# Routing and layer hand-over of a two-layer decoder trunk: where the expert choice keeps its operands, how many tiles it takes at once, in which order the first expert's work is issued, and which engine makes the next mixer's low parts

## The chip, the cores and the metric

One core of one Trainium2 chip. The metric is device time in microseconds of one execution, the median of several runs; lower is better. The engines' names in the profile are PE (TensorE), DVE (VectorE), ACT (ScalarE), POOL (GpSimd) and SP (SyncE, which here issues the weight loads).

## What is computed

Two layers over x of 512 tokens by 1024, float32. In each layer a mixer (attention of several kinds, ending in an output projection), a LayerNorm, a mixture of 16 experts of which every token uses two, and a second LayerNorm. The part that the change touches most is the choice of experts between the first LayerNorm and the experts:

```python
x = layer_norm(ALPHA * x + mix, ln_g[l, 0], ln_b[l, 0])
aff = jax.nn.sigmoid(xt @ router_w)                       # [512, 16]
sel = aff + router_b
grp_score = lax.top_k(sel.reshape(-1, 4, 4), 2)[0].sum(-1)   # best two of four, summed
g_mask = one_hot(top_k(grp_score, 1))                        # the best group
_, e_idx = lax.top_k(where(e_mask, sel, -inf), 2)            # two experts in it
w = take_along_axis(aff, e_idx); w = w / w.sum(-1)
for e in range(16):
    h = silu(xt @ w_gate[e]) * (xt @ w_up[e])
    y = y + gates[:, e:e + 1] * (h @ w_down[e])
x = layer_norm(ALPHA * x + y, ln_g[l, 1], ln_b[l, 1])
```

## The kernel before

**Number format.** Every product is made of three TensorE products of high and low parts (`mm3`): high by high, low by high, high by low. Of each weight unit of 128 by 1024, ACT writes the high part `wh` (L182, a cast) and DVE or POOL the low part `wl`, weight minus high part (L183).

**Tiles.** The 512 tokens are four tiles of 128. Tiles 0 and 1 lie in one buffer, 2 and 3 in another.

**Routing, in each layer.** `out_proj` makes, for each tile and each half of the 1024 columns, 12 matmuls of 128x512 (`half_proj`) into one of two PSUM buffers `ps_a`. DVE adds them to the tile (L572), takes LayerNorm statistics (L573), PE transposes the half (L577), ACT copies it (L579) and PE multiplies it by the router's weights (L581). `tile_ln` then finds one over the standard deviation in ten tiny DVE steps, scales the logits (L587, L588), takes the sigmoid on ACT (L589), and applies the LayerNorm: ACT centres and scales (L590), POOL multiplies by gamma and adds beta (L252, L253; of the last tile DVE does 256 of the columns), and POOL's queue writes the tile to two places in DRAM: x1d (L592), from which the experts' rows are gathered, and yd (L595), to which results are added.

The string ROUTE_ORDER sets the order in which the program is written: before, `y0 l0 y1 l1 y2 l2 y3 l3 r02 r23 r34`, where y is a tile's projection, l its LayerNorm, and r a choice for a range of tiles. A choice (`choose`, L414 to L455) is some 17 DVE steps on scores in SBUF; `slots` (L468 to L480) counts, with PE, which place in its expert's list each token gets, and compares these places with 0 to 95 (L480); `first_rows` (L483 to L491) collects the rows of the first expert by matmuls from the tiles in SBUF. Each engine executes its own instructions in the order in which a scheduler put them at build time; an instruction that waits holds up all that stand behind it on its engine.

**Experts.** `moe` takes the collected rows out of PSUM (`put_rows`), finds for all experts which tokens fill their places (`after_slots`, L494 to L530: the indices idx for the gathers, a one-hot matrix oht that only the last expert needs, a flag that an expert overflowed, weights), gathers rows of the next experts from x1d (L1109) and runs the 16 experts: gate, up, silu times up (L1146), transpose, down, scatter to yd. Weight chunks of 1 MB are loaded by SP's queue (L1101) in the order of the program. The first 16 (AHEAD) go to buffers that are free, or come free, before the experts begin. Later ones use a ring of buffers.

**Hand-over to the next layer.** In `moe`'s tail TAIL_ORDER sets the order: for each tile p adds the last expert's part (L1255), c squares (ACT, L1263), n finds one over the standard deviation (L212 to L228), m and e apply the LayerNorm (L1271, L1276), t transposes the tile for the next mixer. The next mixer's input weights arrive in four units of 128x968; ACT makes their high parts and POOL their low parts (`ksplit(..., G)`, L880, which calls L183).

## Time and profile before

| | |
|---|---|
| runs | 1184.47, 1179.41, 1177.62 us, median 1179.41 |
| profiled execution | 1178.62 us, of which the span is 1176.7 |
| PE busy | 1084.6 us (92%) |
| DVE busy | 938.5 us (80%) |
| ACT busy | 758.4 us (64%) |
| POOL busy | 240.9 us (20%) |
| mean granted TensorE clock | 0.956 |

The span is the time between the first and the last instruction. PE works for 92% of it, so a gain has to come out of the stretches in which PE stands or runs at the lower clock. In the page's 40 slices (29 us each) these are at the routing of layer 0 (slices 9 and 10), the hand-over (slice 20) and the routing of layer 1 (slices 29 and 30). Times in the text below are microseconds from the span's start.

### The profile page before, as it was taken

What the parts mean: (1) busy time and instruction counts of PE and PEld (TensorE: products, weight loads), DVE (VectorE), ACT (ScalarE), POOL (GpSimd) and SP (SyncE); (2) the same over time, 40 slices, a digit from 0 to 9 for tenths busy, and PEclk for the clock granted to TensorE, in tenths of its full rate; (3) what the DMA queues carried; (4) which work ended last, traced back from release to release, by engine and by line L of the source; (5) the groups of instructions that cost most, each with busy time, mean ns of one, the idle gap of its engine ahead of it and who ended that gap; (6) DMA issues with size and microseconds to landing.
All of it is one profiled execution on the core that took longest, in us unless ns stands there. A gap on an engine that the chain in (4) does not pass through costs nothing. (4 is left out here: it accounts for less than half of the span.)

```text
span 1176.7 us, 16647 instructions
## 1 busy us (share of the span) xinstructions
PE 1084.6 (92%) x5775; PEld 810.7 (69%) x5775; DVE 938.5 (80%) x1871; ACT 758.4 (64%) x1221; POOL 240.9 (20%) x199
## 2 busy tenths in 40 slices
...
GB/s 209 118 37 53 99 66 143 203 277 317 306 340 360 349 344 242 350 354 302 219 1 69 71 23 72 109 95 119 302 281 298 335 351 349 345 246 357 368 294 141
DMA packets 139756, 262.24 MB, mean 223 GB/s; under 512 B 11847, under 2 KB 28263, under 8 KB 139664
## 3 DMA queue, kind: packets, MB, share of 16 engines
...
q8 instruction: 47, 0.77, 0.3%
...
## 5 line engine op out<-in xcount | busy, mean ns | idle before, releaser
L183 DVE TENSOR_TENSOR wl<-wraw,wh 128x1024 fp32r<-128x1024 f32 (+1 forms) x422 | 503.0, 1218 | 73.2 <-ACT wh L182 63.9
L182 ACT CAST wh<-wraw 128x1024 fp32r<-128x1024 f32 (+3 forms) x436 | 445.8, 1039 | 148.6 <-PE ps_s L197 62.3
L195 PE MATMUL ps_s<-wh,m 128*96 128x512 f32 (+1 forms) x528 | 207.6, 393 | 1.7 <-ACT m L200 1.7
L196 PE MATMUL ps_s<-wl,m 128*96 128x512 f32 (+1 forms) x528 | 205.8, 390 | 0.6 <-DVE wl L183 0.6
L197 PE MATMUL ps_s<-wh,m 128*96 128x512 f32 (+1 forms) x528 | 204.6, 388 | 0.3 <-DVE m L201 0.2
L197 PEld LDWEIGHTS ps_s<-wh,m 128*96 128x96 f32 x528 | 85.5, 162 | 35.6 <-DVE m L201 1.3
L195 PEld LDWEIGHTS ps_s<-wh,m 128*96 128x96 f32 x528 | 85.8, 163 | 34.5 <-ACT m L200 2.1
L196 PEld LDWEIGHTS ps_s<-wl,m 128*96 128x96 f32 x528 | 85.6, 162 | 32.4 <-DVE wl L183 0.8
L195 PE MATMUL ps_a<-wh,hH 128*96 128x512 f32 x256 | 102.5, 400 | 0.5 <-ACT hH L200 0.5
L196 PE MATMUL ps_a<-wl,hH 128*96 128x512 f32 x256 | 101.2, 395 | 0.8 <-DVE wl L183 0.8
L197 PE MATMUL ps_a<-wh,hL 128*96 128x512 f32 x256 | 99.9, 392 | 0.0
L1184 POOL DMA_INDIRECT yd<-m,idx x30 | 53.1, 1770 | 188.5 <-ACT m L1183 187.5
L195 PE MATMUL ps_a<-wh,XH 128*128 128x512 f32 (+2 forms) x224 | 88.7, 396 | 2.5 <-ACT wh L182 1.3
L197 PE MATMUL ps_a<-wh,XL 128*128 128x512 f32 (+2 forms) x224 | 87.6, 391 | 2.1 <-DVE XL L201 2.1
L196 PE MATMUL ps_a<-wl,XH 128*128 128x512 f32 (+2 forms) x224 | 86.7, 387 | 0.0
L1109 POOL DMA_INDIRECT m<-x1d,idx x30 | 33.1, 1105 | 255.3 <-PE ps_t L1120 225.6
L197 PE MATMUL ps_a<-XH,wl 128*128 128x512 f32 x160 | 64.7, 405 | 0.3 <-DVE wl L183 0.3
L196 PE MATMUL ps_a<-XL,wh 128*128 128x512 f32 x160 | 64.9, 406 | 0.0
L195 PE MATMUL ps_a<-XH,wh 128*128 128x512 f32 x160 | 64.6, 404 | 0.0
L358 ACT ACTIVATE p<-p,nm 128x256 f32<-128x256 f32 (+3 forms) x96 | 50.6, 529 | 18.5 <-DVE nm L353 9.5
L377 ACT COPY pT<-ps_t 128x512 f32<-128x512 f32 (+2 forms) x88 | 43.5, 517 | 28.2 <-PE ps_t L374 27.3
L197 PEld LDWEIGHTS ps_a<-wh,hL 128*96 128x96 f32 x256 | 41.3, 161 | 18.0
...
## 6 DMA issues: line engine op xcount, KB each, us to landing
...
```

The source lines that it names most:

```text
L182: first(A.copy(hv, w))
L183: first(eng.tensor_tensor(out=lv, in0=w, in1=hv.bitcast(F32), op=ALU.subtract))
L195: T.matmul(o, lh, rh, start=first, stop=False)
L196: T.matmul(o, lh, rl, start=False, stop=False)
L197: T.matmul(o, ll, rh, start=False, stop=last)
L358: A.activation(out=pt[h], in_=(pt if bias else Sp)[h], func=AF.Exp, bias=nm[:, h:h + 1], scale=(slopes[0][h] if slopes else 1.0), accum_ou ...
L377: A.copy(d_, s_)
L1109: G.indirect_dma_start(out=xg_of[e], out_offset=None, in_=x1d[:, :], in_offset=bass.IndirectOffsetOnAxis(ap=idx[:CAP, e:e + 1], axis=0), b ...
L1184: G.indirect_dma_start(out=yd[:, :], out_offset=bass.IndirectOffsetOnAxis(ap=idx[:CAP, e:e + 1], axis=0), in_=yos[e % 2], in_offset=None, ...
```

## The change

- **Choice.** The scores, their sums with the bias, the group sums and the chosen indices lie in an unused part of the PSUM bank of the logits (`scratch`), so that in the choice and the slots no DVE step reads two tensors from SBUF (a column of one value for each partition may be there besides). The sum with the bias is made twice, once to PSUM and once to SBUF, and so is the sigmoid. The compare of places is one TENSOR_SCALAR for each tile.
- **Order of routing.** ROUTE_ORDER is `y0 l0 y1 l1 y2 l2 c03 y3 s03 l3 r03`: one choice for tiles 0 to 2 stands ahead of tile 3's second add; nine of the twelve matmuls of a tile's second half stand behind the logits of the half before. Then comes tile 3's choice by itself.
- **LayerNorm.** Tiles 0 and 1 get their statistics from an add that also sums and from a squaring pass on ACT. Tile 3's LayerNorm is done on DVE in two halves (`centre` and `whole`), placed between the steps of its choice; POOL and ACT do nothing for it, and LN1_DVE is gone. In the one-column case the tiny steps of `rsqrt` are TENSOR_SCALAR with two column operands.
- **First expert.** Its gate's high parts are made behind tile 3's sigmoid and its low parts one by one between `whole` and `put_rows` (before: in the routing, between the choices). `after_slots` is cut in three: `slot_tokens` (indices) in the middle of the first gate, `slot_weights` behind the first expert, `for_the_end` (oht, flag) in expert 4.
- **Buffers.** Chunk 7 (second half of expert 1's up weights) is loaded into the buffer of the first gate's second chunk, and is the last of AHEAD. On SP's queue it stands behind the two loads into the buffers of the tiles; before it stood ahead of them. The router's folded weights are made at the end of the mixer and not in the routing.
- **Hand-over.** The next mixer's four low parts are made by DVE behind tile 0's `e` (`w00 w01 w10`, then `w11`), not by POOL; the steps on ACT keep their order.

Tile 2's second half on DVE in layer 0, before, in the order of the engine (L439 to L450 are steps of the choice of tiles 0 and 1; L572 is the add):

```order
L430 TENSOR_REDUCE gm<-pr 128x2
L439 TENSOR_TENSOR gs<-gs,gm 128x8
L440 TENSOR_TENSOR gs<-gs,desc_121 128x8
L441 TENSOR_REDUCE gm_2680<-gs 128x2
L442 TENSOR_TENSOR gs<-gs,gm_2680 128x8
L443 TENSOR_TENSOR sel<-gs,sel 128x32
L448 MAX rm_2686<-sel 128x8 x2
L450 MAX_INDEX ri_2687<-rm_2686,sel 128x8
L572 TENSOR_TENSOR xr_130<-xr_130,ps_a 128x512
L450 MAX_INDEX ri_2687<-rm_2686,sel 128x8
L573 BN_STATS st<-xr_130 128x6
L452 CAST rf_2692<-ri_2687 128x4
```

After: the end of the choice of tiles 0 to 2, then tile 3's second add (L625), slots and the start of its statistics:

```order
L468 TENSOR_TENSOR sel<-gs,ps_s 128x48
L473 MAX rm_2604<-sel 128x8 x3
L475 MAX_INDEX ri_2605<-rm_2604,sel 128x8 x3
L476 CAST ps_s<-ri_2605 128x6
L477 TENSOR_TENSOR O<-io_119,ps_s 128x96
L480 TENSOR_REDUCE M<-O 128x48
L625 TENSOR_TENSOR xr_130<-xr_130,ps_a 128x512
L503 SCALAR_TENSOR_TENSOR sl<-ps_s,M 128x48
L626 BN_STATS st<-xr_130 128x6
L506 TENSOR_SCALAR oh_2320<-slot_117,sl 128x96 x3
L253 BN_AGGR mv<-st 128x2
```

The add of tile 2's second half no longer stands behind a choice; tile 3's stands behind one of three tiles.

The end of the last choice on DVE in layer 0, before (L455 ends it, L480 compares places, L500 to L506 belong to the indices, L201 is the low part of the first expert's rows):

```order
L455 TENSOR_TENSOR M<-O 128x16
L498 TENSOR_TENSOR R<-O,recc 128x128
L478 SCALAR_TENSOR_TENSOR sl<-ps_s,M 128x16
L519 TENSOR_REDUCE flags<-ps_t 128x1
L480 TENSOR_TENSOR oh_2324<-slot_117,sl 128x96
L500 TENSOR_TENSOR pt<-O,sl 128x128
L513 TENSOR_SCALAR eq<-slot_117,sl 128x96
L502 TENSOR_REDUCE pos<-pt 128x8
L506 TENSOR_SCALAR oh<-slot_117,pos 128x96 x4
L460 TENSOR_TENSOR gt<-O,aff 128x128
L201 TENSOR_TENSOR m_2843<-ps_o,m_2843 128x384
L506 TENSOR_SCALAR oh<-slot_117,pos 128x96
```

After (L480 ends the choice, L676 is `centre`, L681 `whole`, L192 a low part of the first gate, L211 that of the rows, L524 the start of the indices):

```order
L480 TENSOR_REDUCE M<-O 128x16
L676 SCALAR_TENSOR_TENSOR xr_130<-xr_130,mv,lnt 128x512
L503 SCALAR_TENSOR_TENSOR sl<-ps_s,M 128x16
L506 TENSOR_SCALAR oh_2320<-slot_117,sl 128x96
L681 SCALAR_TENSOR_TENSOR xr_130<-xr_130,rs_o,lnt 128x512
L192 TENSOR_TENSOR wl<-wraw_2761,wh 128x1024
L681 SCALAR_TENSOR_TENSOR xr_130<-xr_130,rs_o,lnt 128x512
L211 TENSOR_TENSOR m_2788<-ps_o,m_2788 128x384
L192 TENSOR_TENSOR wl<-wraw_2761,wh 128x1024
L211 TENSOR_TENSOR m_2788<-ps_s,m_2788 128x384
L192 TENSOR_TENSOR wl<-wraw_2763,wh 128x1024
L524 TENSOR_TENSOR pt<-O,sl 128x128
```

The four low parts of the gate and half of tile 3's LayerNorm now lie behind the last choice, and the indices behind three of the low parts.

The hand-over on DVE between the layers, before (L214 to L228 are the last steps of the inverse root, L1276 is `e`, L1271 `m`, L201 the low part of the transposed tile):

```order
L214 TENSOR_TENSOR rs_c<-rs_r 128x2
L215 TENSOR_TENSOR rs_c<-rs_c,rs_h 128x2
L228 SCALAR_TENSOR_TENSOR rs_o<-rs_c,rs_r 128x2
L1276 SCALAR_TENSOR_TENSOR xr_5573<-xr_5573,rs_o,lnt 128x1024
L1271 SCALAR_TENSOR_TENSOR xr_5573<-xr_5573,ls,lnt 128x1024
L201 TENSOR_TENSOR XL_5685<-ps_t,XH_5683 128x4x128
L201 TENSOR_TENSOR XL_5686<-ps_t,XH_5684 128x4x128
L1276 SCALAR_TENSOR_TENSOR xr_5573<-xr_5573,rs_o,lnt 128x1024
```

After (L243 to L245, L1426 and L1421 are the same steps, L1444 the low parts of weights):

```order
L224 TENSOR_TENSOR rs_c<-rs_r 128x2
L225 TENSOR_TENSOR rs_c<-rs_c,rs_h 128x2
L245 SCALAR_TENSOR_TENSOR rs_o<-rs_c,rs_r 128x2
L1426 SCALAR_TENSOR_TENSOR xr_5503<-xr_5503,rs_o,lnt 128x1024
L1444 TENSOR_TENSOR wl<-wraw,wh 128x968 x3
L211 TENSOR_TENSOR XL_5628<-ps_t,XH_5626 128x4x128
L211 TENSOR_TENSOR XL_5629<-ps_t,XH_5627 128x4x128
L1444 TENSOR_TENSOR wl<-wraw,wh 128x968
L1421 SCALAR_TENSOR_TENSOR xr_5503<-xr_5503,ls,lnt 128x1024
L1426 SCALAR_TENSOR_TENSOR xr_5503<-xr_5503,rs_o,lnt 128x1024
```

Four low parts have come to DVE between tile 0's and tile 1's `e`; on POOL none is left there.

The diff, cut to what the steps below touch:

```diff
-AHEAD = (2, 3, 4, 0, 1, 5, 6, 8, 9, 10, 12, 13, 7, 14, 11, 15)
-LN1_DVE = (0, 0, 0, 256)
+AHEAD = (2, 3, 4, 0, 1, 5, 6, 8, 9, 10, 12, 13, 14, 11, 15, 7)
...
-ROUTE_ORDER = "y0 l0 y1 l1 y2 l2 y3 l3 r02 r23 r34"
-TAIL_ORDER = ("p00 p10 / p01 c0 p11 c1 m0 n02 e0 m1 t0 e1 p20 p21 c2 t1 p30 p31 c3 m2 n24 e2 m3 t2 e3 t3",
+ROUTE_ORDER = "y0 l0 y1 l1 y2 l2 c03 y3 s03 l3 r03"
+TAIL_ORDER = ("p00 p10 / h0 | h1 p01 c0 p11 c1 m0 n02 e0 w00 w01 w10 t0 w11 m1 e1 p20 p21 c2 t1 p30 p31 c3 m2 n24 e2 m3 t2 e3 t3",
...
+    def scratch(p):
+        return (p[:, 0:64].rearrange("p (t e) -> p t e", e=NE), p[:, 64:128].rearrange("p (t e) -> p t e", e=NE),
+                p[:, 128:144].rearrange("p (t g) -> p t g", g=4), p[:, 144:152].rearrange("p (t c) -> p t c", c=2))
...
-        V.tensor_tensor(out=sel, in0=aff[:, ts_], in1=rb.unsqueeze(1).to_broadcast([128, n, NE]), op=ALU.add)
-        sg = sel.rearrange("p t (g j) -> p (t g) j", j=4)
+        for t in (selp, sel):
+            V.tensor_tensor(out=t, in0=affp, in1=rb.unsqueeze(1).to_broadcast([128, n, NE]), op=ALU.add)
+        sg, sp = (t.rearrange("p t (g j) -> p (t g) j", j=4) for t in (sel, selp))
...
-        V.tensor_tensor(out=pr[:, :, 0:2], in0=sg[:, :, 0:2], in1=sg[:, :, 2:4], op=ALU.add)
+        V.tensor_tensor(out=pr[:, :, 0:2], in0=sg[:, :, 0:2], in1=sp[:, :, 2:4], op=ALU.add)
...
-        return V.tensor_tensor(out=oh0[:, t0:t1], in0=slot1.unsqueeze(1).to_broadcast([128, n, CAP]),
-                               in1=sl[:, t0:t1, 0:1].to_broadcast([128, n, CAP]), op=ALU.is_equal)
+        for i in range(t0, t1):
+            oh = V.tensor_scalar(oh0[:, i, :], slot1, sl[:, i, 0:1], None, op0=ALU.is_equal)
+        return oh
...
+                o = half_proj(rows[c], oH, oL, g, i, end.get("lg") if main and c else None)
...
+        n = NT - 1
+        with tc.issue_after(end["u"].ins):
+            c0 = centre(0)
+        with tc.issue_after(c0.ins):
+            chosen = choose(n, NT, sc)
+        with tc.issue_after(chosen.ins):
+            c1 = centre(1)
+        with tc.issue_after(c1.ins):
+            oh = slots(sl, oh0, n, NT)
...
-            rows += ksplit(ahead.pop(0) if ahead else latent_load(kh), 2, G)
+            rows += ([(hv[:, j, :], lv[:, j, :]) for _, hv, lv in ahead.pop(kh) for j in range(2)] if ahead else
+                     ksplit(latent_load(kh), 2))
...
-                t = xo.tile([128, 2048], F32, name="wraw3", tag=dict(e=eH, E=eL, l=lL, x=lH)[t])
+                t = xo.tile([128, 2048], F32, name="wraw3", tag=dict(e=eH, E=eL, l=eL, x=lH)[t])
...
-        g0 = [ksplit(load("g", 0, c), 2) for c in range(2)]
-        m2 = xo.tile([128, 2, D], F32R, name="m2", tag=eL)
+        m2 = xo.tile([128, 2, D], F32R, name="m2", tag=lL)
...
-        for c in range(2):
-            put_rows(c, ps2[c])
-        after_slots(sl, oht, flag)
-        for e in (1, 2):
-            gather(e)
+        in_turn(lambda: route["whole"](0))
+        route["rows"](0)
+        low_part(0)
+        in_turn(lambda: route["whole"](1))
+        route["rows"](1)
+        route["x1"]()
+        in_turn(lambda: put_rows(0, ps2[0]))
+        low_part(1)
+        in_turn(lambda: put_rows(1, ps2[1]))
+        low_part(2)
+        found = []
+        def between():
+            with tc.issue_after(last_mm[0].ins):
+                in_turn(lambda: found.extend(slot_tokens(sl, route["room"])) or found[0])
+            low_part(3)
+            for i in (1, 2):
+                gather(i)
...
+            if e == 4:
+                with tc.issue_after(act_op[0].ins):
+                    for_the_end(sl, oht, flag)
...
+        def rest(kh, u):
+            w, hv, lv = early_rows[kh][u]
+            keep(V.tensor_tensor(out=lv, in0=w, in1=hv.bitcast(F32), op=ALU.subtract))
```

## Rows read from the trace of the kernel before

**Rows 1.** Busy time of the engines in stretches of 10 us of layer 0: the routing (first two rows) and the experts (last two). The columns are the stretch, its length, the busy time and count of instructions of PE, PEld, DVE, ACT and POOL, then the granted clock, the mean busy share of the DMA engines and GB/s.

```profile
240.00:250.00 10.00, 7.14 (x35) 6.03 (x34) 7.96 (x32) 1.53 (x2) 4.31 (x4) 0.81 0.96 379
...
260.00:270.00 10.00, 6.95 (x43) 6.86 (x43) 8.78 (x40) 1.34 (x2) 5.02 (x4) 0.67 0.95 335
...
440.00:450.00 10.00, 10.00 (x50) 7.17 (x49) 9.45 (x12) 8.49 (x12) 1.00 (x1) 1.00 0.87 279
450.00:460.00 10.00, 10.00 (x48) 7.03 (x47) 9.20 (x9) 8.66 (x11) 1.59 (x1) 1.00 0.46 134
```

**Rows 2.** Timeline of DVE in the routing of layer 0 and its first expert: start, duration, engine, line, operation, operands; in brackets the idle time ahead of it and what ended it.

```profile
239.07 1.73 DVE L419 TENSOR_TENSOR sel<-aff,rb 128x32 f32<-128x32 f32 x1
...
240.92 2.38 DVE L424 TENSOR_TENSOR pr<-sel 128x16 f32<-128x16 f32 x1
...
245.24 0.67 DVE L572 TENSOR_TENSOR xr<-xr,ps_a 128x512 f32<-128x512 f32 x1
...
256.16 0.18 DVE L478 SCALAR_TENSOR_TENSOR sl<-ps_s,M 128x32 f32<-128x32 f32 x1
...
267.48 0.16 DVE L419 TENSOR_TENSOR sel<-aff,rb 128x16 f32<-128x16 f32 x1
...
270.10 0.17 DVE L455 TENSOR_TENSOR M<-O 128x16 f16<-128x16 f16 x1
...
271.74 0.17 DVE L478 SCALAR_TENSOR_TENSOR sl<-ps_s,M 128x16 f32<-128x16 f32 x1 [1.27 <-PE ps_t L518]
...
271.95 0.26 DVE L480 TENSOR_TENSOR oh<-slot,sl 128x96 f32<-128x96 f16 x1
272.13 0.28 DVE L500 TENSOR_TENSOR pt<-O,sl 128x128 f32<-128x128 f16 x1
...
276.61 0.56 DVE L201 TENSOR_TENSOR m<-ps_s,m 128x384 fp32r<-128x384 f32 x1 [0.23 <-ACT m L200]
...
289.62 0.68 DVE L1146 TENSOR_TENSOR sg<-sg,ps_s 96x512 f32<-96x512 f32 x1
```

**Rows 3.** Timeline of POOL in the same stretch.

```profile
240.83 2.44 POOL L253 TENSOR_TENSOR xr<-xr,lnt 128x1024 f32<-128x1024 f32 x1
...
254.29 3.31 POOL L253 TENSOR_TENSOR xr<-xr,lnt 128x1024 f32<-128x1024 f32 x1
...
265.58 1.86 POOL L253 TENSOR_TENSOR xr<-xr,lnt 128x768 f32<-128x768 f32 x1
...
268.33 0.53 POOL L595 DMA_DIRECT2D yd<-xr  x1
279.15 1.08 POOL L1109 DMA_INDIRECT m<-x1d,idx  x1 [10.29 <-DVE eq L528]
```

**Rows 4.** Timeline of PE in the same stretch.

```profile
245.97 0.91 PE L577 MATMUL ps_t<-ident,xr 128*128 128x128 f32 x4 [2.86 <-DVE xr L572]
...
248.39 1.72 PE L581 MATMUL ps_s<-rwgb,yT 128*128 128x16 f32 x8
...
264.11 0.27 PE L514 MATMUL ps_t<-ident,eq 128*96 128x128 f32 x1
...
267.70 1.99 PE L491 MATMUL ps_o<-oh,xr 128*128 128x96 f32 x8 [3.05 <-DVE sel L419]
...
272.36 2.00 PE L491 MATMUL ps_o<-oh,xr 128*128 128x96 f32 x8 [0.62 <-DVE oh L480]
274.14 1.91 PE L491 MATMUL ps_s<-oh,xr 128*128 128x96 f32 x8
...
276.24 0.77 PE L195 MATMUL ps_s<-wh,m 128*96 128x512 f32 x1
```

**Rows 5.** Timeline of all engines at the hand-over from layer 0 to layer 1.

```profile
574.08 9.74 POOL L183 TENSOR_TENSOR wl<-wraw,wh 128x968 fp32r<-128x968 f32 x4 [12.10 <-ACT wh L182]
...
574.36 3.03 DVE L1271 SCALAR_TENSOR_TENSOR xr<-xr,ls,lnt 128x1024 f32<-128x1024 f32 x1 [3.16 <-ACT sq L1263]
575.34 0.19 ACT L1263 ACTIVATION_READ_ACCUMULATOR sq<-xr,ls 128x1 f32 x1
577.31 2.18 DVE L219 TENSOR_SCALAR rs_v<-ls 128x2 f32<-128x2 f32 x1
...
585.11 1.28 DVE L1276 SCALAR_TENSOR_TENSOR xr<-xr,rs_o,lnt 128x1024 f32<-128x1024 f32 x1
...
586.54 1.94 PE L275 MATMUL ps_t<-ident,xr 128*128 128x128 f32 x8 [14.32 <-DVE xr L1276]
...
589.75 1.27 DVE L1276 SCALAR_TENSOR_TENSOR xr<-xr,rs_o,lnt 128x1024 f32<-128x1024 f32 x1
...
597.53 0.17 DVE L219 TENSOR_SCALAR rs_v<-ls 128x2 f32<-128x2 f32 x1
...
599.32 1.28 DVE L1276 SCALAR_TENSOR_TENSOR xr<-xr,rs_o,lnt 128x1024 f32<-128x1024 f32 x1
```

**Rows 6.** The page's group of the low parts made by DVE: busy time, mean ns of one.

```profile
L183 DVE TENSOR_TENSOR wl<-wraw,wh 128x1024 fp32r<-128x1024 f32 (+1 forms) x422 | 503.0, 1218 | 73.2 <-ACT wh L182 63.9
```

**Rows 7.** What SP's queue waited for at the weight loads (L1101) between 226 and 300: us in total, times, longest.

```profile
SPq L1101 <- DMA yd<-xr: 10.3, 1, 10.3
```

**Rows 8.** Timeline of all engines in layer 1, at the places that answer to 245.97 and 289.62 of layer 0.

```profile
834.72 0.66 PE L577 MATMUL ps_t<-ident,xr 128*128 128x128 f32 x4 [2.98 <-DVE xr L572]
...
878.59 0.68 DVE L1146 TENSOR_TENSOR sg<-sg,ps_s 96x512 f32<-96x512 f32 x1
```

254 lines of the change are left out of this document (176 added, 78 removed).

## The prediction

> **What bounds the kernel now.** I read first the stretches of 10 us [rows 1]. In the experts PE is busy for 10.00 of 10 us at the full clock, so nothing that happens beside them shortens them. In the routing PE is busy for 7.14 and 6.95 of 10, at a granted clock of 0.81 and 0.67. There the timelines of DVE, POOL and PE are laid side by side [rows 2 to 4]. The reader is to see three things. First, the add of tile 2's second half (L572 at 245.24) stands on DVE behind a choice that was held up: L419 took 1.73 and L424 2.38, where an undisturbed L419 takes 0.16 [rows 2]. L424 ends at 243.30, POOL's L253 at 243.27 [rows 2, 3]. Both held steps read two tensors from SBUF; L478 at 256.16, which reads PSUM and one tensor from SBUF, took 0.18 in the middle of a POOL step (254.29 to 257.60). PE waited 2.86 us for that add and then ran the logits at the low clock: 1.72 for eight [rows 4]. Second, DVE begins the last choice only at 267.48, just after POOL has finished tile 3 (267.44) [rows 2, 3], and PE stands for 3.05 [rows 4]. Third, from the end of that choice (270.27) to the first gate product (276.24) everything is a chain: slots, the last tile's rows for the first expert, their split. At the hand-over PE stands for 14.32 us [rows 5], since DVE's steps are held while POOL makes four low parts from 574.08 to 583.82. So DVE's queue sets the time at all three places.
>
> **The change part by part.** Times are those of the trace before; the steps that I place are estimates.
>
> Routing of layer 0. Without a choice ahead of tile 2's add the 2.86 us go, and tile 2's logits end at 250.1 - 2.9 = 247.2. Two scalings and a sigmoid later, at about 248.5, the choice of three tiles starts. The choice of one tile took 267.48 to 270.27, 2.8 us [rows 2]; three tiles add four searching steps, one sum and some width, which I put at 1.3: it ends at 252.6. Tile 3's second add stands behind it on DVE, and behind that add PE's transposes and logits; PE, which has nine matmuls in hand, runs dry at about 250.4 and stands for about 2.5 us. Because a stop of 2.86 was followed by the low clock, I reckon with that clock behind this one. Add, slots, statistics and the ten tiny steps of the root (1.75 undisturbed, 597.53 to 599.28 [rows 5]) bring tile 3's scores to about 257.3 and the last choice to 258.0, with half of `centre` ahead of it. It takes 2.9, to 260.9. From the choice's end to the slots there are 1.5 us (270.27 to 271.74), with the other half of `centre` hidden in them; compare 0.26 and `whole` 0.7 give 263.4. The rows of the last tile take 2.0 and 1.9 on PE [rows 4]; the first gate product comes at 267.4 instead of 276.24. POOL's LayerNorm of tile 3, which ended at 267.44, is no longer in the way; its two halves on DVE cost 0.7 each, of which one lies in a wait.
>
> First expert. Now DVE is the bound, because the gate's four low parts have moved behind the choice. From 263.4: four low parts of the gate at 1.22 [rows 6] 4.9, the second `whole` 0.7, the rows' low parts two at 0.56 [rows 2] 1.1, the indices (three steps at 0.28, two of 128x384 at about 0.56, and a wait of some 1.0 for PE's eight small matmuls) 3.0, four low parts of up 4.9, about 1.0 of waits for ACT: 15.6, to 279.0. The last unit's matmuls add 1.5: the product L1146 starts at about 280.9 with some slack, against 289.62 [rows 2]. I take a gain of **8.5 us**. The bound below the chain is PE: 48 matmuls, of which it does some 50 in 10 us where nothing else holds it [rows 1], so not before about 278.5, a gain of 11. The bound above is 5: steps held once more, and a late gather.
>
> Two waits are new here. POOL's gather for expert 1 needs the indices (about 272.5, before 278.7) and tile 3's rows in DRAM, which POOL's queue now writes at about 266 (yd at 268.33 before [rows 3]). SP waited 10.3 us for such a write [rows 7]. I place the gather at 275 and its landing at 279; the rows are wanted at 281, so it costs nothing, with 2 us of cover. And the compares of places, as TENSOR_SCALAR, stand on DVE ahead of tile 3's statistics while POOL still works on tile 2. TENSOR_SCALAR steps are not safe: one of 128x2 at 577.31 took 2.18 beside POOL [rows 5]. Held at worst once, they cost up to 2.4; POOL should end tile 2 near 254.7, just as they are due, so I take 0.5, which is in the slack above.
>
> The Trainium skill (SBUF — State Buffer, "Who interferes with whom") says that a DVE step with at most one SBUF input stays clear of GpSimd, but that tensor_scalar can enter a mode that takes the shared ports and then blocks. The trace agrees with both halves (0.18 for L478, 2.18 for L219); by it the compares would wait for POOL, and the sum would be up to 3 us worse over both layers than with none held.
>
> The Trainium skill also speaks against putting the choice in PSUM: Perfetto Trace Analysis, "Optimizing Scalar/DVE Operations", gives about 60 ns of access overhead for DVE on SBUF and about 125 on PSUM. Here L478, which reads PSUM, took 0.17 and L419 from SBUF 0.16, so the trace doesn't bear it out for reads; writes to PSUM no row shows. By the skill's figure some 18 steps in each layer would cost 65 ns more, an estimate of 1.2 us a layer, and the sum would come out at 1161.
>
> Layer 1. The same chain: from PE's stop to the product are 43.9 us (834.72 to 878.59 [rows 8]), in layer 0 43.65. I take the same 8.5.
>
> Hand-over. `m` started at 574.36 and the squares end at 575.53; undisturbed, the root runs to 577.4 instead of 585.0, and `e` of tile 0 to 578.7 instead of 586.4: 7.7 earlier. But then four low parts stand on DVE. At 1.22 x 968/1024 = 1.15 each they cost 4.6, of which part lies in waits for the transposes' split (about 0.9 before). Tile 1's `e` ends at about 587.0 against 591.0, and the same chain follows to tile 2's `e` (599.32). I take **4.0**. Bounds: 7.7 - 4.6 = 3.1, and 6, the gain of the first products, if what follows catches up. The casts on ACT stay ahead of the squares as before.
>
> Added to the experts. The one-hot matrix and the flag are made in expert 4, where PE has no idle time: eight small matmuls and transposes, 0.27 long at 264.11 but overlapping [rows 4]; between 0.3 and 1.5, I take **0.5 a layer**. The squares of tiles 0 and 1 on ACT cost nothing: ACT is busy for 1.53 of 10 [rows 1]. The fold of the router's weights lies at the mixer's end, beside PE's work.
>
> Weights. Expert 0 starts 8.5 us earlier, and the loads must follow. In the experts the DMA engines are full but for 440 to 460, with shares of 0.87 and 0.46 [rows 1]: 1.3 + 5.4 = 6.7 us in which they had no free buffer. That is the stream's slack; the missing 1.8 comes out of the lead of some chunks. I cost it at nothing.
>
> Sum: -8.5 - 8.5 - 4.0 + 1.0 = -20.0 against the profiled execution's 1178.6 (span 1176.7): 1158.6. The runs' median is 0.8 higher; I say **1159**.
>
> **The rivals.** (a) The loads don't follow. If the stretch from 460 on is bound by the DMA and not by buffers, both layers end as before and only the hand-over is left: 1178.6 - 4 + 1 = 1176. Against it: PE is busy for 10.00 of 10 while the DMA pauses. (b) The choice is held after all, because a DVE step that writes PSUM or reads a column beside POOL waits as L424 did. A choice of three tiles beside POOL's four steps would lose up to 4 us a layer: 1158.6 + 8 = 1167. (c) All goes better: the clock stays high behind PE's shorter stop and DVE keeps up: 2.5 more a layer and 2 at the hand-over, 1151. (d) Slower: chunk 7. On SP's queue it now stands behind the load into tile 2 and 3's buffer, and that one waits for the write of tile 3's rows. The write starts at about 266 and lands some 11 us later, 277.4; two loads of 1 MB at some 340 GB/s [rows 1] take 6.2, so chunk 7 lands at 283.6. It is wanted at about 286.5 (first expert's end 281 plus a gate of 5.5). From a landing of the write at 280.3 on, each us costs one in each layer; the kernel gets slower than before when the write takes 13 us more. At 26 us instead of 11 it would be 12 late: 2 x (12 - 8.5) - 4 + 1 = +4, 1183. (e) The change doesn't do what it says, PE's three stops stay: 1178.
>
> **How the numbers follow.** My forecast 0.69, (a) 0.06, (b) 0.10, (c) 0.09, (d) 0.04, (e) 0.02. The forecast's own bounds are 5 to 11 a layer, 3.1 to 6 at the hand-over and 0.3 to 1.5 of added work: 1151 to 1168. The range takes in those and most of (b) and (c): 1150 to 1170. About 0.5% (6 us) is what a measurement of this kernel can tell from no change; faster by more than that are my forecast, (b) and (c), 0.88; within it (a) and (e), 0.08; slower (d), 0.04.
>
> **What would show it.** Right: no DVE step of the choice over 0.4 us while POOL works; the last choice on DVE 9 to 10 us earlier relative to tile 2's transposes; first gate product and L1146 8 to 9 us earlier in both layers; PE's stop at the hand-over 6 to 8 us instead of 14.32; rows of PE in expert 4 longer by about 0.5. Wrong: a choice step of 2 us, PE idle ahead of the first expert's matmuls waiting for DVE by more than 3 us in all, ACT or DVE waiting for a weight load in expert 1, or a wait of expert 1's transposes for the gather.

## The result and the profile after

The changed kernel took 1193.56 us in the median of 4 runs (1188.42 to 1199.26), the kernel before 1179.14 beside it; the ratio is 1.0106, with a 95% interval of [1.0078, 1.0133] (it compares runs taken beside each other, here and below, and isn't the quotient of the medians, which is 1.0122). The forecast was 1159, with a range of 1150 to 1170: the sign was wrong. The profiled execution is the longest of the four, 1199.26 (span 1197.1), so its stages add up to more than the median shows. One of the nine runs of e9 below took 1757.1 us at a granted clock of 0.55; it is in none of the figures.

Spans of the two traces, cut at the same events. "Routing" runs from the first transposes of tile 0's new rows (L577, now L630) to the first gate product of expert 0; "first expert" from there to the product of activation and up of expert 1 (the second L1146 of a layer, now L1257).

| us | before | after | difference |
|---|---|---|---|
| start to the routing of layer 0 | 222.07 | 224.46 | +2.4 |
| routing, layer 0 | 54.17 | 48.83 | -5.3 |
| first expert, layer 0 | 27.82 | 40.42 | +12.6 |
| other experts of layer 0 | 253.98 | 254.34 | +0.4 |
| hand-over and mixer of layer 1 | 255.80 | 253.88 | -1.9 |
| routing, layer 1 | 49.94 | 50.71 | +0.8 |
| first expert, layer 1 | 29.26 | 38.95 | +9.7 |
| other experts of layer 1 | 252.29 | 254.24 | +1.9 |
| end | 31.37 | 31.27 | -0.1 |

So the loss lies in the two first experts. Stretches of 10 us in layer 0, columns as in [rows 1]:

```profile
250.00:260.00 10.00, 5.01 (x22) 4.46 (x23) 5.11 (x33) 1.80 (x4) 7.16 (x7) 0.61 0.33 130
...
270.00:280.00 10.00, 8.14 (x35) 6.32 (x35) 8.20 (x15) 2.51 (x4) 1.05 (x2) 0.66 0.83 257
...
290.00:300.00 10.00, 5.11 (x32) 3.91 (x31) 5.93 (x12) 5.09 (x7) 5.15 (x3) 0.83 1.04 351
```

In two of these stretches PE is busy for half of the time, and DVE, which the forecast took for the bound there, for 5.11 and 5.93 us. DVE's timeline, which answers to [rows 2]:

```profile
252.14 0.22 DVE L444 TENSOR_TENSOR ps_s<-ps_s,rb 128x48 f32<-128x48 f32 x1 [0.31 <-ACT ps_s L652]
...
254.57 0.33 DVE L473 MAX8 rm<-sel 128x8 f32<-128x16 f32 x3
...
255.86 0.25 DVE L480 TENSOR_REDUCE M<-O 128x48 f16<-128x96 f16 x1
261.89 0.69 DVE L625 TENSOR_TENSOR xr<-xr,ps_a 128x512 f32<-128x512 f32 x1 [5.78 <-PE ps_a L207]
...
266.89 0.18 DVE L444 TENSOR_TENSOR ps_s<-ps_s,rb 128x16 f32<-128x16 f32 x1
...
269.64 0.19 DVE L480 TENSOR_REDUCE M<-O 128x16 f16<-128x32 f16 x1
...
270.79 0.74 DVE L681 SCALAR_TENSOR_TENSOR xr<-xr,rs_o,lnt 128x512 f32<-128x512 f32 x1
...
276.66 0.56 DVE L211 TENSOR_TENSOR m<-ps_s,m 128x384 fp32r<-128x384 f32 x1 [1.70 <-ACT m L210]
...
283.22 0.17 DVE L538 TENSOR_SCALAR idx<-ps_s 96x16 uint32<-96x16 f32 x1 [3.09 <-PE ps_s L536]
...
284.45 4.62 DVE L183 TENSOR_TENSOR wl<-wraw,wh 128x1024 fp32r<-128x1024 f32 x4
...
294.27 0.29 DVE L543 TENSOR_TENSOR og<-O,gates 128x128 f32<-128x128 f16 x1
296.14 0.68 DVE L1257 TENSOR_TENSOR sg<-sg,ps_s 96x512 f32<-96x512 f32 x1 [1.57 <-ACT sg L1254]
```

The choice of three tiles (252.14 to 256.11) works as forecast: no step over 0.33, though POOL works beside it from 253.45 on (its line is below). But the add of tile 3's second half then waits 5.78 us for PE. PE's timeline, against [rows 4]:

```profile
255.97 1.86 PE L634 MATMUL ps_s<-rwgb,yT 128*128 128x16 f32 x8 [4.99 <-DVE O L477]
...
271.59 1.13 PE L517 MATMUL ps_o<-oh,xr 128*128 128x96 f32 x8 [1.29 <-DVE xr L681]
273.29 0.74 PE L205 MATMUL ps_s<-wh,m 128*96 128x512 f32 x1 [0.57 <-ACT m L210]
...
284.58 0.47 PE L206 MATMUL ps_s<-wl,m 128*96 128x512 f32 x1 [1.39 <-DVE wl L192]
...
294.62 1.53 PE L547 MATMUL ps_t<-og,yT 128*96 128x16 f32 x16 [3.30 <-DVE og L543]
297.75 1.54 PE L1227 MATMUL ps_t<-ident,m 96*128 96x96 f32 x8 [1.60 <-DMA m<-x1d,idx]
```

PE stands for 4.99 us ahead of the logits of tile 3's first half, released by L477, a step of the choice; the nine matmuls for which DVE waits are queued behind these logits. Later it stands 1.39 for a low part of the gate, 3.30 for `og` (L543), the gates' weights by slot, and 1.60 for the rows that POOL gathers for expert 1. POOL's timeline, against [rows 3]:

```profile
253.45 2.33 POOL L269 TENSOR_TENSOR xr<-xr,lnt 128x1024 f32<-128x1024 f32 x1 [1.80 <-ACT xr L663]
...
273.63 0.53 POOL L668 DMA_DIRECT2D x1d<-xr  x1 [13.99 <-DVE xr L681]
...
284.27 7.08 POOL L1216 DMA_INDIRECT m<-x1d,idx  x1 [9.59 <-DVE idx L538]
```

The gather's issue takes 7.08 us, before 1.08; DVE runs low parts beside it, four of them without a gap (284.45 to 289.07). On ACT, expert 0's activation waits for the matmuls of the gates' weights, since the one-hot rows that these read lie in its two buffers:

```profile
295.51 0.59 ACT L1254 ACTIVATE sg<-ps_s 96x512 f32<-96x512 f32 x1 [1.80 <-PE ps_t L547]
```

The whole first expert of layer 0, before (first line) and after, in the columns of [rows 1]:

```profile
276.24:304.06 27.82, 26.78 (x140) 19.25 (x140) 23.41 (x38) 20.67 (x25) 4.03 (x3) 0.99 0.84 285
273.29:313.71 40.42, 34.13 (x158) 24.98 (x159) 27.15 (x37) 20.82 (x24) 12.45 (x5) 0.84 0.83 269
```

Of the 12.6 us that it grew, PE stands for 5.3 (6.29 after, 1.04 before). For the other 7.35 it works longer: it has 18 matmuls more, and its granted clock is 0.84 instead of 0.99. In layer 1 it stands for 3.2 us more and works for 6.5 more, at 0.82 instead of 0.94. Behind the stops of 3.30 and 1.60, from 296.14 to 313.71, the clock is 0.81 in the mean, so part of that stretch ran at the low level (1.2 GHz) and not at 2.4.

Layer 1, all engines, against [rows 8], shows the same stops but the one for the gathered rows:

```profile
853.74 1.86 PE L634 MATMUL ps_s<-rwgb,yT 128*128 128x16 f32 x8 [4.99 <-DVE O L477]
...
859.66 0.69 DVE L625 TENSOR_TENSOR xr<-xr,ps_a 128x512 f32<-128x512 f32 x1 [5.78 <-PE ps_a L207]
...
882.27 5.99 POOL L1216 DMA_INDIRECT m<-x1d,idx  x1 [8.24 <-DVE idx L538]
...
893.70 2.58 PE L547 MATMUL ps_t<-og,yT 128*96 128x16 f32 x16 [2.79 <-DVE og L543]
...
895.66 0.68 DVE L1257 TENSOR_TENSOR sg<-sg,ps_s 96x512 f32<-96x512 f32 x1 [2.02 <-ACT sg L1254]
```

The hand-over, all engines, against [rows 5]:

```profile
583.49 1.90 ACT L1438 CAST wh<-wraw 128x968 fp32r<-128x968 f32 x2 [6.94 <-DMA wraw<-in_odd_w_in_dram]
585.29 1.14 ACT L1413 ACTIVATE sq<-xr,ls 128x1024 f32<-128x1024 f32 x1
...
586.63 1.28 DVE L1421 SCALAR_TENSOR_TENSOR xr<-xr,ls,lnt 128x1024 f32<-128x1024 f32 x1 [6.62 <-ACT sq L1413]
...
589.68 1.28 DVE L1426 SCALAR_TENSOR_TENSOR xr<-xr,rs_o,lnt 128x1024 f32<-128x1024 f32 x1
590.88 3.31 DVE L1444 TENSOR_TENSOR wl<-wraw,wh 128x968 fp32r<-128x968 f32 x3
...
591.11 1.94 PE L292 MATMUL ps_t<-ident,xr 128*128 128x128 f32 x8 [10.56 <-DVE xr L1426]
...
607.12 1.28 DVE L1426 SCALAR_TENSOR_TENSOR xr<-xr,rs_o,lnt 128x1024 f32<-128x1024 f32 x1
```

POOL is out of the way (root and `e` of tile 0 follow the scaling at once), but DVE now waits 6.62 us for ACT's squares, and these stand behind casts that wait 6.94 for their weights.

### The profile page after: what moved, and what is told of

It is laid out like the page before. It is cut to its first block, busy times and chain, and to the rows that moved or that the text cites. A ratio compares the mean times of both kernels' runs of the same rounds, so it can differ in the third digit from the quotient of the medians.

```text
span 1197.1 us, 16624 instructions
## 1 busy us (share of the span) xinstructions
PE 1097.9 (92%) x5787; PEld 819.2 (68%) x5787; DVE 918.0 (77%) x1827; ACT 762.3 (64%) x1235; POOL 229.5 (19%) x191
## 4 chain that ended last, share of the span: by engine, by line
PE 75%; DVE 12%; DMA 6%; ACT 4%; issue 3%; POOL 0%; DVEq 0%; SPq 0%; ACTq 0%; POOLq 0%
PE ps_a L207 10%; PE ps_a L206 10%; PE ps_a L205 10%; PE ps_s L205 9%; PE ps_s L207 9%; PE ps_s L206 9%; PE ps_o L398 3%; PE ps_t L391 3%; DMA wraw<-in_odd_w_in_dram 2%; PE ps_t L1227 2%; DMA wraw<-in_moe_w_up_dram 1%; PE ps_s L1112 1%; ACT wh L182 1%; PE ps_s L341 1%; DVE wl L183 1%
## 5 line engine op out<-in xcount | busy, mean ns | idle before, releaser
L183 DVE TENSOR_TENSOR wl<-wraw,wh 128x1024 fp32r<-128x1024 f32 (+2 forms) x414 | 492.2, 1216 | 75.5 <-ACT wh L182 66.9
L182 ACT CAST wh<-wraw 128x1024 fp32r<-128x1024 f32 (+1 forms) x424 | 433.8, 1039 | 150.4 <-PE ps_s L207 75.4
L205 PE MATMUL ps_s<-wh,m 128*96 128x512 f32 (+1 forms) x528 | 209.8, 397 | 1.1 <-ACT m L210 1.1
L207 PE MATMUL ps_s<-wh,m 128*96 128x512 f32 (+1 forms) x528 | 208.2, 394 | 0.0
L207 PEld LDWEIGHTS ps_s<-wh,m 128*96 128x96 f32 x528 | 86.9, 165 | 35.5 <-issue 0.6
L205 PEld LDWEIGHTS ps_s<-wh,m 128*96 128x96 f32 x528 | 86.9, 165 | 34.7 <-ACT m L210 1.9
L205 PE MATMUL ps_a<-wh,h 128*96 128x512 f32 x256 | 102.4, 400 | 1.0 <-ACT h L210 1.0
L206 PE MATMUL ps_a<-wl,h 128*96 128x512 f32 x256 | 100.9, 394 | 0.1
L207 PE MATMUL ps_a<-wh,h 128*96 128x512 f32 x256 | 100.8, 395 | 0.0
L1216 POOL DMA_INDIRECT m<-x1d,idx x30 | 44.0, 1465 | 252.2 <-PE ps_t L1227 233.4
L375 ACT ACTIVATE p<-p,nm 128x256 f32<-128x256 f32 (+3 forms) x96 | 50.6, 529 | 16.3 <-DVE nm L370 8.5
L207 PEld LDWEIGHTS ps_a<-wh,h 128*96 128x96 f32 x256 | 41.3, 161 | 17.8
```

The source lines that it names most:

```text
L182: first(A.copy(hv, w))
L183: first(eng.tensor_tensor(out=lv, in0=w, in1=hv.bitcast(F32), op=ALU.subtract))
L205: T.matmul(o, lh, rh, start=first, stop=False)
L206: T.matmul(o, lh, rl, start=False, stop=False)
L207: last_mm[0] = T.matmul(o, ll, rh, start=False, stop=last)
L375: A.activation(out=pt[h], in_=(pt if bias else Sp)[h], func=AF.Exp, bias=nm[:, h:h + 1], scale=(slopes[0][h] if slopes else 1.0), accum_ou ...
```

## The experiments

The theory after reading the trace: **the bank**. The scores lie in the PSUM bank of the logits, PE doesn't write there while DVE works on the choice, and the nine matmuls behind pay for it; 8 us a layer. Its rivals are the hand-over from expert 0 to expert 1 (weights by slot, activation's buffer, gather) and the low parts of the first expert's gate, which the change puts behind the last choice (**order of use**). Ratios are to the kernel before, which ran beside each. R and X are routing and first expert as in the table above, from each run's trace, layer 0 / layer 1. The diffs are cut to the lines that matter.

| kernel | median, us | ratio | R | X |
|---|---|---|---|---|
| before | 1179.14 | 1 | 54.2 / 49.9 | 27.8 / 29.3 |
| changed | 1193.56 | 1.0106 [1.0078, 1.0133] | 48.8 / 50.7 | 40.4 / 39.0 |
| e1_nine_free | 1191.74 | 1.0092 [1.0056, 1.0128] | 49.3 / 47.8 | 37.1 / 38.8 |
| e2_own_bank | 1191.35 | 1.0067 [1.0042, 1.0092] | 46.4 / 48.7 | 38.7 / 37.1 |
| e3_choice_sbuf | 1194.13 | 1.0081 [1.0040, 1.0123] | 51.0 / 50.6 | 38.5 / 36.0 |
| e4_weights_later | 1194.32 | 1.0117 [1.0063, 1.0171] | 48.8 / 50.6 | 38.0 / 38.6 |
| e5_weights_room | 1195.52 | 1.0103 [1.0071, 1.0135] | 50.4 / 50.7 | 39.5 / 39.6 |
| e7_gather_first | 1189.40 | 1.0063 [1.0040, 1.0086] | 49.3 / 50.7 | 39.0 / 36.4 |
| e10_gate_early | 1183.87 | 1.0006 [0.9984, 1.0029] | 53.4 / 52.8 | 30.2 / 31.5 |
| e13_early_bank | 1184.61 | 1.0040 [1.0025, 1.0056] | 52.6 / 53.4 | 30.0 / 29.1 |
| e12_early_bank_room | 1186.79 | 1.0070 [1.0044, 1.0096] | 53.6 / 50.9 | 29.3 / 31.5 |
| e16_two_one | 1191.70 | 1.0079 [1.0058, 1.0100] | 55.1 / 54.3 | 32.1 / 31.2 |
| e14_before_in_use | 1191.37 | 1.0079 [1.0054, 1.0105] | 56.7 / 54.4 | 30.4 / 29.9 |
| e17_before_psum | 1182.52 | 0.9999 [0.9981, 1.0017] | 54.7 / 52.1 | 27.5 / 27.5 |
| e9_handover_alone | 1177.68 | 0.9939 [0.9915, 0.9962] | 53.3 / 51.1 | 28.6 / 29.1 |
| e20_casts_behind | 1171.82 | 0.9928 [0.9900, 0.9957] | 53.3 / 53.0 | 28.6 / 28.1 |

R and X come from one execution each. The kernel before, e9 and e20 have the same routing and first expert, and their R differs by up to 3.0 us (49.9, 51.1 and 53.0 in layer 1) and their X by up to 1.2; the changed kernel, e4, e5 and e7 share a routing, and their R differs by 1.6 (48.8 to 50.4 in layer 0). So a difference of one to three us in one column shows little by itself.

**The bank** (four runs).

```diff
 e1   o = half_proj(rows[c], oH, oL, g, i, end.get("lg") if main and c
-         else None)
+         and i < NT - 1 else None)
 e2
-    sc = scratch(bank[:, 2 * NT * NE:512])      # and slots(): pp = ps_s()
+    sc = scratch(ps_s())                        # and slots(): pp = bank[:, 128:512]
 e3
+    sc = scratch(sm.tile([128, 152], F32, name="scr", bufs=1))
```

> Changed kernel, but the nine later matmuls of tile 3's second half are not kept behind tile 3's first logits. Theory 'bank': the scores and the choice lie in the PSUM bank of the logits, so tile 3's logits (and whatever is queued on TensorE behind them) stand until the choice of three tiles has ended; without the hold TensorE works through its nine matmuls in that time, VectorE's second add comes ahead of or into the choice instead of 5.78 us late, and the last choice starts about 7 us earlier in each layer: some 14 us less than the changed kernel, about 1179. The stop of 4.99 us before the logits shrinks to 1 or 2, since they still wait for the choice. Rival 'loads': the first experts are bound by the weight stream or by the gather, and what the routing gains is waited for there: within 3 us of the changed kernel, with a longer wait in expert 1.

> Changed kernel, but the scores and the choice lie in a PSUM bank of their own, and the slots' small sums in the logits' bank instead; the nine matmuls stay held behind the logits. Theory 'bank': the stop of 4.99 us before tile 3's logits goes, the add of tile 3's second half no longer waits 5.78 us for TensorE, the last choice starts some 8 us earlier in each layer, the time falls by 14 to 16 us to about 1177. Rival 'loads': within 3 us of the changed kernel. Rival 'hold': the logits wait for something else that the choice does (its last write of the one-hot rows, or the scratch as such): the stop stays at about 5 us and the time stays.

> Changed kernel, but the scores and the operands of the choice lie in SBUF; all else as in the changed kernel. Theory 'bank': the stop before tile 3's logits goes as with a bank of its own, and the routing gains the same 8 us a layer less what GpSimd holds VectorE up: 1177 if no step is held, up to 4 us a layer more (1185) if two or three steps of 2 us are. If PSUM operands were what kept the choice quick, steps of the choice of 1.7 to 2.4 us show beside GpSimd's steps of 128x1024; if not, none over 0.4. Rival 'loads': 1192 as before.

The mechanism is as told: with a bank of their own, or in SBUF, the scores release the logits, and no wait for L477 is left in either layer (in e1, where they share the bank, 3.74 us of it are left). The price isn't: R and X together fall by 4.2 and 3.9 us in e2, and by 3.0 and 3.0 in e1, where 7 to 8 a layer were expected. In time neither can be told from the changed kernel, since the intervals overlap. All engines of e2 in layer 0:

```profile
255.90 1.04 PE L634 MATMUL ps_s<-rwgb,yT 128*128 128x16 f32 x8 [1.42 <-DVE u L650]
...
263.66 5.37 PE L517 MATMUL ps_o<-oh,xr 128*128 128x96 f32 x24 [0.75 <-DVE oh L506]
...
268.86 2.85 PE L517 MATMUL ps_s<-oh,xr 128*128 128x96 f32 x24
...
271.83 0.17 DVE L503 SCALAR_TENSOR_TENSOR sl<-ps_s,M 128x16 f32<-128x16 f32 x1 [3.12 <-PE ps_s L501]
```

The last choice came earlier, but its slots now wait 3.12 for PE, which does the 48 row matmuls of three tiles in one go, in 8.2 us of work. Is that the next bound? e18 takes 32 of the 48 away (so that expert 0 lacks the rows of tiles 0 and 1).

```diff
-                for i in range(t0, t1):
+                for i in range(max(t0, t1 - 1), t1):
```

> Changed kernel with a bank of its own for the choice (as in the second run), and of the three tiles' rows for the first expert, which stand on TensorE between the slots of tiles 0 to 2 and the sums for the last slots, only one tile's: 16 matmuls of 48 and 16 (the first expert then lacks the rows of tiles 0 and 1). Theory 'rows in one go': with the bank repaired, TensorE's 48 matmuls (5.37 and 2.85 us in layer 0 of that run) are what the last slots wait for (3.12 us on VectorE); without 32 of them that wait goes and the first gate product comes 3 to 5 us earlier in each layer: some 6 to 9 us less than with a bank alone. Rival 'VectorE': the last choice sets the slots' time anyway: nothing gained, within 2 us.

With the other rows an expert got more than its 96 slots, and the kernel's guard computed both layers again by its dense path: the 4580.84 us of this run say nothing, but its two layers ahead of that can be read. R falls from e2's to 45.3 and 45.0, by 1.0 and 3.7; X grows to 39.1 and 41.0, and the sum is lower by 0.7 in layer 0 and higher by 0.3 in layer 1. So what is saved in the routing here is lost again in the first expert.

In e3 two steps of the choice are held in each layer, each about as long as the POOL step beside it (all engines):

```profile
254.37 2.36 POOL L269 TENSOR_TENSOR xr<-xr,lnt 128x1024 f32<-128x1024 f32 x1 [2.77 <-ACT xr L663]
254.53 2.23 DVE L465 TENSOR_TENSOR scr<-scr,desc 128x12 f32<-128x12 f32 x1
...
256.81 2.35 POOL L270 TENSOR_TENSOR xr<-xr,lnt 128x1024 f32<-128x1024 f32 x1
...
256.99 2.19 DVE L467 TENSOR_TENSOR gs<-scr,gm 128x12 f32<-128x12 f32 x1
```

So the premise of the change holds: operands in PSUM saved DVE 4.1 us a layer here (0.18 and 0.17 for the same two steps in the changed kernel). R of e3 is longer than that of e2 by 4.6 and 1.9.

**Expert 0 to expert 1** (three runs). Each adds to the one before: e5 keeps the one-hot rows in the tile of the hidden rows, e7 holds DVE until the gather is issued.

```diff
 e4   if e < last:
          rows_in(e + 1)
+     if e == 0:                                 # moved from ahead of rows_in
+         with tc.issue_after(put.ins):
+             slot_weights(found[1])
 e5
-            oh = room()[:, 0:4 * CAP].rearrange("p (j s) -> p j s", j=4)
+            oh = oh_of[:, h]     # oh_of: a tile of tag "h"
 e7
+            gather(1)
+            with tc.issue_after(got[0].ins):
+                G.memset(ticks[:, 0:1], 0.0)
+            in_turn(lambda: V.tensor_copy(ticks[:, 1:2], ticks[:, 0:1]))
             low_part(3)
-            for i in (1, 2):
-                gather(i)
+            gather(2)
```

> Changed kernel, but the gates' weights by slot (eight small matmuls and the steps ahead of them) are written behind the transposes of expert 1's rows instead of ahead of them. Theory 'queue': the waits of 3.30 and 2.79 us on TensorE ahead of those eight matmuls go, and what is left of them is the rows' wait for the gather (1.60 in layer 0): 3 us less in layer 0 if the rows have landed by then, 1 if not, 3 in layer 1: 4 to 6 us less than the changed kernel, about 1187. Rival 'gather': the rows land only when the wait ends now, so nothing is gained: within 2 us.

> Changed kernel, the eight matmuls of the gates' weights written behind expert 1's transposes, and the one-hot rows that they read kept in the buffer of the hidden rows instead of in the two buffers of the activation, so that expert 0's activation needn't wait for them. Theory 'hand-over to expert 1': between the end of expert 0's matmuls and expert 1's transposes lie three limits one behind the other, the weights' eight matmuls, the activation's buffer, and the gather. With two of them gone the third stays: TensorE waits 3 to 4 us for the gathered rows in each layer; 6.4 and 5.2 us (changed kernel) become 3.5; the first product of expert 1 comes 2.5 and 1.5 us earlier: about 4 us less than the changed kernel. Rival 'gates only': the eight matmuls were all that held it, the rows have long landed: nothing is left of the stop, 11 us less.

> As the kernel with the weights later and the one-hot rows in a buffer of their own, and in addition VectorE stands still behind the indices until GpSimd has issued expert 1's gather (a tiny GpSimd step behind the gather, read by a tiny VectorE step). Theory 'held gather': GpSimd's issue of the gather (7.08 and 5.99 us in the changed kernel, 1.08 before) takes as long as VectorE's low parts of 128x1024 run back to back beside it; with VectorE still it takes about 1.1 us, the rows land some 5 us earlier, TensorE doesn't wait for them, and what the pause costs (about 2.3 us of VectorE, the last low part of the gate and the four of up 2.3 us later) is less than the stop that goes: rows' transposes right behind expert 0's last matmul, the first product of expert 1 about 2 us earlier than without the pause. Rival 'slow transfer': the issue's length is the transfer's own (96 rows by index while weights stream): it stays at 5 to 7 us and the pause only adds 2 to 6 us a layer.

Taking away the weights and the buffer gained nothing in time: in e5 PE waits 6.75 and 4.05 us for the gathered rows alone, and from 292 to 300 the granted clock is 0.50, the low level. The gather itself can be freed; all engines of e7:

```profile
281.30 0.17 DVE L538 TENSOR_SCALAR idx<-ps_s 96x16 uint32<-96x16 f32 x1 [1.93 <-PE ps_s L536]
...
282.35 1.08 POOL L1219 DMA_INDIRECT m<-x1d,idx  x1 [8.30 <-DVE idx L538]
...
283.59 0.15 DVE L1350 COPY ticks<-ticks 128x1 f32<-128x1 f32 x1 [2.12 <-POOL ticks L1349]
...
283.74 1.98 POOL L1219 DMA_INDIRECT m<-x1d,idx  x1 [0.18 <-issue]
...
284.93 0.74 PE L206 MATMUL ps_s<-wl,m 128*96 128x512 f32 x1 [3.67 <-DVE wl L192]
...
289.40 0.42 PE L1230 MATMUL ps_t<-ident,m 96*128 96x96 f32 x1 [2.02 <-DMA m<-x1d,idx]
```

With DVE still, the issue takes 1.08 (in layer 1 too), and the rows are there 8.1 us behind the indices (281.30 to 289.40), in the changed kernel 14.5 (283.22 to 297.75). So the issue was held by DVE's low parts, and wasn't the transfer's own length. The pause costs PE 3.67 us ahead of the gate's last unit, and X is shorter than in e5 by 0.5 and 3.2; the ratio is 1.0063 against 1.0103, with intervals that overlap. The late gather alone is therefore not the whole loss: with it freed, X is still 39.0 and 36.4.

**Order of use** (two runs that answer each other): the changed kernel without it, and the kernel before with it alone.

```diff
 e10
-        with tc.issue_after(route["act"].ins):   # and low_part(j): in turn
             raws = [...]
+        for w in raws:
+            units.append(high(w))
+            low(w, *units[-1][0:2])
 e14
+            with tc.issue_after(oh.ins):         # oh: the last slots, then the low part before
+                oh = V.tensor_tensor(out=lo, in0=w, in1=hi.bitcast(F32), op=ALU.subtract)
```

> Changed kernel, but the first expert's gate is split into high and low parts as early as before (beside the routing, wherever VectorE and ScalarE are free) and not in order of use behind the last choice. Theory 'order of use': four low parts of 1.22 us between the last choice and expert 0's product are what makes the first expert long (from its first gate product to its last matmul 18.0 and 18.3 us, before 13.3 and 14.8) and what makes the indices late (9.9 and 8.6 us behind the first gate product, before 2.5 and 3.8): without them 14 us and 5 us, the gather is issued 4 us earlier, and the first product of expert 1 comes 4 to 6 us earlier in each layer, less 1 to 3 us that the steps cost in the routing: 4 to 8 us less than the changed kernel, about 1187. Rival 'bank': the first expert is only late because the routing is: no gain, and with the low parts in the routing 0 to 5 us more.

> The kernel before, with one part of the change alone: the low parts of the first expert's gate one behind the other after the last choice's slots, not beside the choice. Theory 'order of use': four low parts of 1.22 us stand between the last choice and expert 0's rows and indices: the first gate product comes no earlier, expert 0 ends and the indices come 4 to 5 us later in each layer, 8 to 10 us more than the kernel before, about 1190. Rival 'bank': order of use costs nothing without the bank's stop: within 2 us of the kernel before.

Both come out as this theory said, e10 by more than it expected (1.0% of the time, some 12 us, where 4 to 8 were). Without the order of use, R and X together are 5.6 and 5.4 us shorter in the two layers, and the ratio falls from 1.0106 to 1.0006; with it alone, the kernel before is 5.1 us longer in each layer, and its ratio is 1.0079. In e10 the indices come 5.8 us behind the first gate product (9.9 in the changed kernel), and the gather's issue is short (1.96 in layer 1); POOL and DVE:

```profile
283.57 0.17 DVE L538 TENSOR_SCALAR idx<-ps_s 96x16 uint32<-96x16 f32 x1 [0.38 <-PE ps_s L536]
...
285.76 1.08 POOL L1216 DMA_INDIRECT m<-x1d,idx  x1 [7.80 <-DVE as__2920 L489]
```

PE's stop at the bank is still there (4.96). It hardly matters: two repairs at once, and the choice in pieces again, are told by three runs (e13 and e12 are e10 with e2's and e5's edits, e16 is e13 with `ROUTE_ORDER = "y0 l0 y1 l1 c02 y2 s02 l2 r02 c23 y3 s23 l3 r23"`).

> Changed kernel with both repairs that moved something: the first expert's gate split as early as before, and the scores and the choice in a PSUM bank of their own. Theory 'two costs': the order of use and the shared bank cost separately; the bank's repair takes another 4 to 5 us a layer off the kernel with the early gate alone (as it took 4.2 and 3.9 off the changed kernel up to expert 1's first product): the stop of 4.96 us before tile 3's logits goes, the time is 1174 to 1177 where the kernel before has 1180, ratio about 0.995. Rival 'one chain': VectorE is what bounds the routing once the low parts are back in it, and the stop before the logits only moves to the add of tile 3's second half: no gain over the early gate alone, 1183.

> As the kernel with the early gate and a bank of its own, and in addition the eight matmuls of the gates' weights behind expert 1's transposes with their one-hot rows in the hidden rows' buffer. Theory 'hand-over to expert 1': with the indices early enough the rows have landed when expert 0's matmuls end, so the stop ahead of expert 1's transposes (1.1 to 2.9 us with the early gate alone) goes: 1 to 2 us a layer less than without. Rival 'held gather': the rows land no earlier, the stop stays at 1 to 4 us as a wait for the transfer: nothing gained.

> Kernel with the early gate and a bank of its own, but the choice as before in three pieces (tiles 0 and 1, then 2, then 3), each followed by its slots and rows; operands in PSUM. Theory 'rows in one go': the rows of tiles 0 and 1 (32 matmuls) are done beside tile 2 and 3, where TensorE stood anyway; the last slots no longer wait for 48 matmuls: the first gate product 2 to 4 us earlier in each layer, 1176 to 1179 against 1180 before. Rival 'VectorE': a choice more costs VectorE 2.6 us, and the add of the next tile's half waits for it as in the kernel before: 0 to 3 us a layer more than with three tiles at once, 1185 to 1190.

e13 brings 1.0 and 1.7 us in R and X, which is within what traces differ by, and nothing in the time. PE's stop ahead of the logits stays 3.75 and 4.23 us, now released by L650, DVE's read of tile 2's logits from the same bank, which stands behind one of the gate's low parts: the rival was right that nothing is gained, though the stop did not move to the add. e12 brings nothing. e16 is worse than e13 in both layers, and in time (1.0079 against 1.0040): three tiles at once is not the loss.

**What the prediction rested on**: the held steps, with the hand-over (e17), and the hand-over alone (e9).

```diff
 e9   # before, with cast, rest and run of the changed kernel
-TAIL_ORDER = ("p00 p10 / p01 c0 p11 c1 m0 n02 e0 m1 t0 e1 ...
+TAIL_ORDER = ("p00 p10 / h0 | h1 p01 c0 p11 c1 m0 n02 e0 w00 w01 w10 t0 w11 m1 e1 ...
 e17  # e9, with scratch and choose of the changed kernel
+    bank = ps_s()
+    sc = scratch(ps_s())
-                choose(i, j)
+                choose(i, j, sc)
```

> The kernel before with two parts of the change: the hand-over (low parts on VectorE) and the choice's operands in PSUM, here in a bank of their own; pieces of the choice, gate and experts as before. Theory 'held steps': the 1.73 and 2.38 us that two steps of the choice took beside GpSimd in the kernel before go, TensorE's stop of 2.86 us shrinks to about 0.5 in each layer, the hand-over gives 3 to 4: 1171 to 1174, ratio 0.992. Rival 'next late': what comes behind the choice is bound by GpSimd's LayerNorm of tile 3 or by TensorE, so the held steps cost nothing in the end: as the hand-over alone, 0.994 to 0.997.

> The kernel before with one part of the change: the next mixer's first four low parts on VectorE behind tile 0's normalised rows, their casts behind the last weights' product, in place of GpSimd's four low parts. All else as before. Theory of the prediction: 4.0 us less than before (bounds 3.1 and 6). From the trace of the changed kernel, where the offset fell by 3.1 across this stretch: 3 us less, about 0.25%. Rival: the third load of the next mixer's weights, which no longer waits for GpSimd, takes bandwidth from the second half of the first ones; with the old order of work that costs all of it: 0.

e17 is no faster than the kernel before. PE's 2.86 went, but the order of the program came out another way, and PE stands once a layer, for 10.14 and 10.90 us (at 270.50 in layer 0, for L463, the choice's last step): this run doesn't price the held steps by themselves. R was 54.7 and 52.1, so at best nothing was gained. e9 is faster than both kernels. The stretch from the last product of activation and up in layer 0 to the last tile's `e` is 42.2 us, before 45.2, in the changed kernel 43.0. In time e9 gains 0.6% (0.4 to 0.9), some 7 us, so its trace places only 3.0 of them.

e20 moves ACT's casts of the second weights behind the squares:

```diff
- "... / h0 | h1 p01 c0 p11 c1 m0 n02 e0 ..."
+ "... / h0 | p01 c0 p11 c1 h1 m0 n02 e0 ..."     # cast(1): issue_after(the last square)
```

> The kernel before with the hand-over of the change alone, and ScalarE's casts of the second half of the next mixer's first weights written behind the squares of tiles 0 and 1 instead of ahead of them. Theory 'casts ahead': in the changed kernel and in the hand-over alone these casts wait 6.5 to 6.9 us on ScalarE for their load, and the squares, which need no load, stand behind them; so VectorE stands 6.2 to 6.6 us and the hand-over gained 2 to 3 us where 4 were forecast. With the squares ahead, VectorE's first scaling starts some 4 us earlier (at about 2 us behind the second half's statistics), the first normalised rows come 3 to 4 us earlier, and what is late next is the casts and their low parts: 1 to 3 us less than the hand-over alone by the last tile's rows, ratio 0.991 to 0.994. Rival 'load': the low parts that the next mixer's products need come from the same load, so TensorE waits for those: nothing gained against the hand-over alone.

```profile
569.47 1.15 ACT L1265 ACTIVATE sq<-xr,ls 128x1024 f32<-128x1024 f32 x1 [2.52 <-DVE ls L1263]
...
570.81 1.28 DVE L1273 SCALAR_TENSOR_TENSOR xr<-xr,ls,lnt 128x1024 f32<-128x1024 f32 x1 [0.40 <-ACT sq L1265]
...
573.28 1.90 ACT L1290 CAST wh<-wraw 128x968 fp32r<-128x968 f32 x2 [1.30 <-DMA wraw<-in_odd_w_in_dram]
...
573.86 1.28 DVE L1278 SCALAR_TENSOR_TENSOR xr<-xr,rs_o,lnt 128x1024 f32<-128x1024 f32 x1
...
575.29 1.94 PE L275 MATMUL ps_t<-ident,xr 128*128 128x128 f32 x8 [3.86 <-DVE xr L1278]
```

PE's stop shrinks to 3.86, and the stretch to 36.3 us: 8.9 less than before, where the theory expected 4 to 6. At 1171.82 it has the lowest median of all; by the ratios it can't be told from e9.

## Why the prediction was wrong

- **The routing.** Right: the choice in PSUM isn't held, takes 4.0 us (252.14 to 256.11; forecast 4.1), and the last choice 2.9. (One step, MAX_INDEX, does name two SBUF tensors, `rm` and `sel`, unlike what the section on the change says; it shows as pairs of instructions of 0.07 and 0.17 us at L475, beside POOL, and isn't held.) Wrong: "PE, which has nine matmuls in hand, runs dry at 250.4". The nine were queued behind logits that waited for the choice; the diff shows that hold (`behind`) and the shared bank (`bank[:, 2 * NT * NE:512]`). The first gate product came 5.3 us earlier in layer 0 and 0.8 later in layer 1, forecast 8.8 in both. The traces price the bank at about 4 us a layer while the gate is in order of use, and at 1 to 2, within their spread, without; by the ratios of e2 and the changed kernel it is some 2 a layer, not clear of noise.
- **The first expert**, the term that turned the sign. From the first gate product to expert 0's product of activation and up the sum gave 13.5 us (267.4 to 280.9), as before (13.4); it took 22.9 (273.29 to 296.14). The sum did put the four low parts of the gate into DVE's chain, and the chain took 17.5 instead of 15.6 (from the end of `whole` at 271.53 to 289.07, with waits of 1.70 and 3.09 where 2.0 stood in the sum). It left out what hangs on that chain: 7.1 us passed from its end to the product instead of 1.9, since the weights by slot, which weren't costed at all, and the activation's buffer lie there. The indices, placed 5.1 us behind the first gate product, came 9.9 behind it, 2.5 before. "I place the gather at 275 and its landing at 279 ... it costs nothing, with 2 us of cover" was the step that failed on the way to expert 1: issued at 284.27, held by DVE, landed at 297.75. X became 12.6 and 9.7 us longer instead of equal. e10 and e14 show 5 us a layer for the order of use from both sides. The waits took each other's place (e4, e5, e18), so that I can't give each its share; but over half of what X grew is PE working longer, with 18 matmuls more and at a granted clock of 0.84 and 0.82. The prediction reckoned with the low clock behind a stop in the routing, and not here. Without the order of use (e10) PE stands in X for 1.4 and 1.9 us, and the clock is 0.94 and 0.93.
- **The hand-over.** POOL's 9.74 us went as forecast, and tile 0's rows came sooner. "The casts on ACT stay ahead of the squares as before" named the place and missed its price: before, the weights were there at 571.21; now the casts wait 6.94 for them. PE's stop became 10.56 us, where 6 to 8 were to show it. The gain was 2.2 to 3.0 by the traces, forecast 4.0 (e9's time says some 7, at least 4); the trace of e20 shows that it could have been 8.9.
- **Expert 4** grew by 0.7 a layer (18.39 and 18.35 between its products and expert 3's, 17.68 before), forecast 0.5. **The weights** cost nothing, as forecast: no wait for a weight load in expert 1.
- **The rivals.** (a) to (e) all missed it. A slower outcome was given 0.04, for a late chunk 7; what came was a wait for an index. Two of the signs that the prediction had named as wrong did show: PE idle for DVE ahead of the first expert (4.99 and 1.29 us), and a wait of expert 1's transposes for the gather (1.60, in layer 0 alone).
- **Open:** with gate and bank repaired, and with the hand-over of the change (e13), the changed kernel is still 0.4% slower than the kernel before, though the hand-over alone makes that one 0.6% faster. Expert 4 gives 1.4 us of it, R and X of layer 1 some 3.3, which is hardly more than traces differ by; no run tells what in the new routing costs these.
